# A planner's transfer time, own-result delay and margins renewed, and side work that joins excursions, in a decoder layer

## The chip, the cores and the metric

The kernel runs on one core of a Trainium2 chip. The metric is the device time of one execution in microseconds. Before the change three runs gave 2277.83, 2268.82 and 2278.66 us, with a median of 2277.83 us. One more execution was recorded by the hardware profiler and took 2273.33 us, of which the instructions span 2271.4 us.

## The reference

One decoder layer over 1024 tokens, with 16 learned tokens put in front (1040 columns). All of it is float32.

```python
def swiglu(h, w_gate, w_up, w_down):
    return (jax.nn.silu(h @ w_gate) * (h @ w_up)) @ w_down
...
h = jnp.concatenate([meta, x], axis=1)
n = rms_norm(h, ffn1_norm[l])
h = h + 0.5 * swiglu(n, ffn1_w_gate[l], ffn1_w_up[l], ffn1_w_down[l])
n = rms_norm(h, mix_norm[l])
proj = n @ w_in[l]
...
sb_out = stick_breaking_attention(q, k, v)
rw_out = rwkv7_time_mix(proj[..., 3 * SB_WIDTH:], ...)
h = h + jnp.concatenate([sb_out, rw_out], axis=-1) @ w_out[l]
n = rms_norm(h, ffn2_norm[l])
h = h + 0.5 * swiglu(n, ffn2_w_gate[l], ffn2_w_up[l], ffn2_w_down[l])
return rms_norm(h, final_norm)[:, N_META:]
```

The model width is 1024 and the hidden width of the two feed-forward blocks is 2816. The attention has 8 heads of 64, and so has the recurrence (RWKV-7), which carries a 64 x 64 state per head through all tokens.

## The kernel before

**Tiling.** Activations lie transposed, features on the 128 partitions and tokens along the free axis. The tokens fall into group A (16 learned tokens and the first 512) and group B (the last 512). The long matrix products are the *dense* work: first feed-forward, input projection, output projection, second feed-forward, each for A and then for B. Each float32 product is made of three matmuls in a reduced-precision format (`mm3`, L640): the weight block and the activation are each split into a high and a low part (`whi`, `wlo`; `nh`, `nl`), and high x high, high x low, low x high are summed in PSUM. A weight block comes in by one DMA of 512 KB (`wraw`), ScalarE writes `whi`, and VectorE writes `wlo`. Two such pairs are held at a time, so a new one is split when an old one has been used up. PSUM tiles tell the stage: `pd` is a projection or a down product, `pg` a gate, `pu` (with `nh` and `nl`) an up product, `pwo` the output projection. In the first feed-forward of A and the second of B a part of the products is done in a scheme with fewer multiplications (`quad`), in which the weights also pass through sums on GpSimd.

**Side work.** Beside the dense stream run smaller tasks that also need TensorE: the recurrence and the attention of a group, and the norms. In the recurrence, `lanes` (L1509) inverts small triangular blocks in the steps `pw`, `pp`, `pz`, `pe`. `chain` (L1598) then goes through the token chunks in order; each chunk has a `px<-rsv,x`, a `pu<-us,tt` and a `px<-rsv,bg`, and between two of these ScalarE and VectorE copy a result out of PSUM (into `us`, into `rsv`), without which the next can't start. In the norms, `nps` sums squares and `nyp` spreads the root over the partitions. The attention has `pz`, `pat` and `po`. When TensorE leaves the dense stream for side work, that is called an excursion here.

**What sets the order.** All engines' programs are written out in full when the kernel is built. A planner (`Clock`, L186) keeps a model of the time of each engine and lets tasks go on in the order of the model: the dense task has priority 0, `chain` 9, `lanes` 7, the recurrence's preparation 6 and its end 5, attention 4 to 2, norms 12, weight loads and splits 41 and 40. A task that needs data tells so with `Need` (L141); its `at` (L152) gives the modelled time at which the data are there, plus a margin from `SLACK` (L37) for its priority. `Clock.run` (L400) takes the task that can start first, and at equal times that with the higher priority; the dense task has no margin. Operations of the other engines are held back and committed in the order of the modelled time (`catch_up`, L375; `issue`, L349). So a number of the model changes no instruction, only where each stands in its engine's queue. On the chip each engine works through its queue in that order and waits at an instruction whose data aren't there.

**The output projection of B** needs the recurrence and the attention of B. `plan` (L1225) and `poll` (L2337) put it into the second feed-forward of A, ahead of the first gate that is planned after the data of B are there, or behind that block.

Of the kernel before, what the change touches and what calls it, by code (L numbers as in the profile page):

```python
# [23 lines left out]
NFT = FF // P  # L24
# [9 lines left out]
DB = 2  # L34
WOFF = 1500
NL = 3
SLACK = {9: 0.05, 8: 0.08, 7: 1.5, 6: 0.4, 5: 0.4, 4: 0.4, 3: 0.15, 2: 0.2, 12: 0.1}  # L37
GB = 2
BUFS = [dict(raw=2, qs=4, kh=4, vs=2, sg=8, f=3, at=4, z=2, t=2, o=1),
        dict(raw=1, qs=4, kh=4, vs=2, sg=8, f=2, at=4, z=2, t=2, o=1)]  # L40
WOUT = ((0, 1, 2, 3, 4, 5, 6, 7, 4, 5), (0, 1, 2, 3, 4, 5, 6, 7))
QF = 6
AHEAD = 0.1
BACKLOG = 3.0
PARTS = [(0, 2), (2, 6), (6, 10), (10, 14), (14, 18), (18, 22)]

# [26 lines left out]
class Op:  # L73
# [3 lines left out]
    def at(self):  # L77

        t = self.start
        for d in self.deps:  # L80
            if d.end is None:
                return None
            t = max(t, d.end)
        return t


# [54 lines left out]
class Need:  # L141


    def __init__(self, clk, aps, bank, slack):
        self.clk, self.aps, self.bank, self.slack = clk, [(x.name, Clock.box(x)) for x in aps], bank, slack
        self.both = False

    def __add__(self, t):
        self.slack += t
# [2 lines left out]
    def at(self):  # L152
        t = self.clk.written(self.aps)
        if t is not None and self.bank:
            pool, *ring = self.bank() if callable(self.bank) else self.bank
            f = pool.free(*ring)
            if self.both and f is not None:
                g = pool.free(ring[0], ring[1] - 1)
                f = None if g is None else max(f, g)
            t = None if f is None else max(t, f)  # L160
        return None if t is None else t + self.slack


class Task:
# [21 lines left out]
class Clock:  # L186
# [8 lines left out]
    def __init__(self):  # L195
        self.pe, self.task, self.tasks, self.urg, self.ahead, self.seq = 0.0, None, [], 0, False, 0
        self.clk = dict(v=0.0, a=0.0, g=0.0, s=0.0)
        self.dma = self.port = 0.0
        self.pend = {e: [] for e in self.clk}
        self.wr, self.rd, self.free, self.live, self.held = {}, {}, {}, {}, set()  # L200
        self.mode, self.fast, self.busy = None, True, set()

    @staticmethod
    def box(ap):
# [52 lines left out]
    def cost(self, eng, op, out, ins, k):  # L257

        n = 1
        for d in out.shape[1:]:  # L260
            n *= d
        if eng == "v":
            for x in ins if op == "tensor_reduce" else ():
                n = max(n, x.shape[1] * (x.shape[2] if len(x.shape) > 2 else 1))
            return 0.11 + n * 1e-3 * (2.2 if op == "tensor_tensor_scan" else 8 if op == "reciprocal" else 1.11), 0.17
        if eng == "a":
            far = len(out.shape) > 2 and out.ap[-1][0] * 4 > 64
            return 0.08 + n * 0.84e-3 * (2.2 if far else 1), 0.19
        if eng == "g":
            return ((0.1 + n * 0.85e-3 if op == "memset" else 0.2 + n * 0.9e-3 if op == "affine_select" else 0.22 + n * 1.7e-3), 0.12)  # L270
        if eng == "s":
            big = out if out.space != DRAM or not ins else ins[0]
            m = big.shape[0]
            for d in big.shape[1:]:
                m *= d
            run = min(x.shape[-1] if x.ap[-1][0] == 1 else 1 for x in [out] + ins)
            return 0.3, m * 4 / 2.4e5 * (1 if run >= 128 else 2)
        return self.pe_cost(out, ins, k.get("rhs"), n), 0.23

    def pe_cost(self, out, ins, rhs, n):  # L280
# [20 lines left out]
    def trace(self, eng, op, call, out, ins, k):  # L301
        T = self.task
        o = Op()
        o.eng, o.call, o.task, o.end = eng, call, T, None
        o.cost, o.lat = self.cost(eng, op, out, ins, k)
        lvl = self.LOAD if self.ahead else self.URGENT if self.urg > 0 else self.LAZY if self.urg < 0 else self.PLAIN
        self.seq += 1
        o.port = eng == "g" and op != "memset" or eng == "v" and op.startswith(("tensor_tensor", "scalar_tensor")) and \
            all(x.space != PSUM for x in ins)
        o.prio, o.seq, o.start = (-lvl, -T.prio, self.seq), self.seq, max(self.pe, self.free.get(out.name) or 0.0)  # L310
        deps = {}
        for x in ins:
            b = self.box(x)
            for q, w in self.wr.get(x.name, ()):
                if self.hit(q, b):
                    deps[id(w)] = w
            self.rd.setdefault(x.name, []).append((b, o))
        outs = [out] + [k[n] for n in ("accum_out",) if n in k]
        for x in outs:
            b = self.box(x)  # L320
            if x.space != DRAM:
                for m in (self.wr, self.rd):
                    l = m.get(x.name, ())
                    for q, w in l:
                        if w is not o and self.hit(q, b):
                            deps[id(w)] = w
                    if l:
                        m[x.name] = [(q, w) for q, w in l if w is o or not self.inside(q, b)]
            self.wr.setdefault(x.name, []).append((b, o))
        o.deps = [d for d in deps.values() if eng != "pe" or d.eng != "pe"]  # L330
        o.names = {x.name for x in ins + outs}
        for x in o.names:
            self.live.setdefault(x, []).append(o)
        if eng == "pe":
            for d in o.deps:
                if d.end is None:
                    self.issue(d)
            o.start = max(o.at(), self.pe)
            self.pe = o.start + o.cost
            o.end = self.pe + o.lat  # L340
            o.deps = o.call = None
            T.t = max(T.t, o.end)
            call()
        else:
            self.pend[eng].append(o)
            if not T.free:
                T.ops.append(o)

    def issue(self, o):  # L349
# [7 lines left out]
            self.port = self.clk[o.eng]  # L357
        if o.eng == "s":
            self.dma = max(self.dma, o.start + 0.3) + o.lat
            o.end = max(self.dma, o.start + 0.3 + o.lat) + 1.9  # L360
        else:
            o.end = o.start + o.cost + o.lat
        self.pend[o.eng].remove(o)
# [88 lines left out]
class Ker:  # L452
# [403 lines left out]
    def ffn(self, nm, h, n, chunks, edge, bank, first=None, hook=None, wx=False, poll=None, resid=None, done=None, wy=False, fast=False, once=False):  # L856
# [127 lines left out]
        for part in PARTS:  # L984
            f0, f1 = part
# [48 lines left out]
            if f1 == NFT and hook:  # L1034
                yield from last(part)
            elif not (fast and f1 >= QF):
                for q in range(f1 - f0):
                    yield from downs(part, q)
        for op, x, f in quad_order() if fast else ():
            if op == "d":  # L1040
# [184 lines left out]
    def plan(self):  # L1225

        F = self.flags
# [11 lines left out]
        def ffn(nm, poll=False, wx=False, fast=False, once=False):  # L1239
# [7 lines left out]
            for f0, f1 in PARTS:  # L1247
# [16 lines left out]
                if f1 < NFT:  # L1264
# [1 line left out]
                        F["woutat"] = f1  # L1266
                        yield from wout(True)
                    yield gu("gate", f1)
                yield from [down(f0, f1, q) for q in range(f1 - f0)]
            for op, x, f in quad_order() if fast else ():  # L1270
                if op == "d":
                    yield down(*x, f)
# [785 lines left out]
    def body(self):  # L2058
# [59 lines left out]
        ck, F = self.clock, self.flags  # L2118
# [179 lines left out]
        def director():  # L2298
            yield lambda: F.get("first") and F.get(("xb", 2)) and F.get(("xb", 3)) and F.get(("root", 0, 1)) and F.get("fast1") and psp.quiet()
            psp.release()  # L2300
            for g in range(2):
# [21 lines left out]
                self.ap.release()  # L2323
                self.psa.release()
                F["mix", g] = True
            f2b = f2["p"] = pool("f2b", bufs=1, side="right")
            f2["x"] = self.wx = pool("f2x", bufs=1, side="right")
            ext.extend((pool("psF2", bufs=1, space=PSUM), "e", 6 - DB))
# [144 lines left out]
```

## Time and profile before

| | us |
|---|---|
| three runs | 2277.83, 2268.82, 2278.66 (median 2277.83) |
| profiled execution | 2273.33 |
| its span | 2271.4 |
| DVE (VectorE) busy | 1566.0 (69%) |
| ACT (ScalarE) busy | 1085.4 (48%) |
| POOL (GpSimd) busy | 555.8 (24%) |

In the rows of the profile PE is TensorE, DVE VectorE, ACT ScalarE, POOL GpSimd and SPq the queue that issues DMAs. "L101" is the line of the helper that issues every operation, so instructions are told apart by their tiles, out<-in. PEclk is the share of TensorE's full clock that the chip granted. Matmuls overlap, so what one of them costs is read from start to start, and an idle time of TensorE stands in brackets with what ended it.

### The profile page before, as it was taken

How to read it: one execution, taken by the hardware profiler on the slowest of the kernel's cores; microseconds unless marked ns; L12 is line 12 of the kernel's file. 1: busy time of each engine (PE TensorE's matmuls, PEld its weight loads, DVE VectorE, ACT ScalarE, POOL GpSimd, SP SyncE). 2: the span in 40 equal slices, each digit the busy share in tenths (PEclk: the TensorE clock that was granted, in tenths of full speed). 3: DMA queues.
4: the chain of work that ended last, by engine and by line, in shares of the span. 5: the costliest groups of instructions: out<-in, count | busy, mean ns of one | idle time of the engine just before them, and what ended most of it. 6: DMA issues, size and time to landing. Idle time of an engine off the chain costs nothing.

```text
span 2271.4 us, 41476 instructions
## 1 busy us (share of the span) xinstructions
PE 2239.5 (99%) x16303; PEld 1979.7 (87%) x16303; DVE 1566.0 (69%) x2673; ACT 1085.4 (48%) x2157; POOL 555.8 (24%) x700
## 2 busy tenths in 40 slices
PE   8999999999999999999999999999999999999998
PEld 7999999999878888778788987887877899899998
DVE  6888887475666655676476877547777656688885
ACT  6444444434343534555434554445666335354444
POOL 1322120013133231431012415324443001231110
PEclk9999999999999999999999989999999999999999
DMA  5543332545633233322545524333221433333332
GB/s 166 180 112 103 93 94 78 170 132 145 182 105 106 74 100 98 100 88 67 172 141 175 159 79 128 86 92 116 76 85 52 144 112 126 91 109 109 105 90 78
DMA packets 407384, 256.54 MB, mean 113 GB/s; under 512 B 44941, under 2 KB 392293, under 8 KB 407190
## 3 DMA queue, kind: packets, MB, share of 16 engines
q1 hardware_dynamic: 407190, 253.90, 38.2%
q8 instruction: 128, 2.10, 0.4%
q14 instruction: 66, 0.54, 0.1%
HBM read 219.85 MB, written 33.99 MB: 112 GB/s over the span
## 4 chain that ended last, share of the span: by engine, by line
PE 94%; DVE 2%; ACT 1%; DMA 1%; issue 1%; SPq 0%; POOL 0%; DVEq 0%; ACTq 0%; POOLq 0%
PE pd L101 34%; PE pu L101 22%; PE pg L101 21%; PE pwo L101 4%; PE px L101 3%; PE po L101 2%; PE pz L101 2%; PE pat L101 2%; PE pG L101 1%; DVE wlo L101 1%; PE psw L101 0%; DMA wraw<-in_ffn_w_gate_dram 0%; SPq L101 0%; PE pp L101 0%; ACT whi L101 0%
## 5 line engine op out<-in xcount | busy, mean ns | idle before, releaser
L101 ACT ACTIVATE whi<-wraw 128x1024 fp32r<-128x1024 f32 x314 | 330.6, 1053 | 333.9 <-PE pd L101 208.8
L101 DVE TENSOR_TENSOR wlo<-wraw,whi 128x1024 fp32r<-128x1024 f32 (+1 forms) x312 | 401.0, 1287 | 88.6 <-ACT whi L101 83.8
L101 PE MATMUL pd<-ah,whi 128*128 128x512 f32 (+2 forms) x944 | 325.9, 345 | 2.6 <-DVE h L101 1.2
L101 PE MATMUL pd<-ah,wlo 128*128 128x512 f32 (+2 forms) x944 | 319.3, 338 | 1.2 <-DVE wlo L101 1.2
L101 PE MATMUL pd<-al,whi 128*128 128x512 f32 (+2 forms) x944 | 318.5, 337 | 0.1
L101 PE MATMUL pd<-nh,whi 128*128 128x256 f32 (+7 forms) x648 | 210.6, 325 | 0.3 <-DVE st L101 0.2
L101 PE MATMUL pu<-nh,whi 128*128 128x512 f32 (+3 forms) x576 | 207.0, 359 | 0.0
L101 PE MATMUL pd<-nl,whi 128*128 128x256 f32 (+7 forms) x648 | 204.5, 316 | 0.0
L101 PE MATMUL pd<-nh,wlo 128*128 128x256 f32 (+7 forms) x648 | 204.4, 315 | 0.0
L101 PE MATMUL pg<-nh,whi 128*128 128x512 f32 (+3 forms) x536 | 199.8, 373 | 0.5 <-ACT nh L101 0.5
L101 PEld LDWEIGHTS pd<-ah,whi 128*128 128x128 f32 x944 | 177.6, 188 | 25.5 <-issue 3.1
L101 PE MATMUL pu<-nh,wlo 128*128 128x512 f32 (+3 forms) x576 | 198.6, 345 | 0.6 <-DVE wlo L101 0.6
L101 PE MATMUL pu<-nl,whi 128*128 128x512 f32 (+3 forms) x576 | 198.7, 345 | 0.0
L101 PEld LDWEIGHTS pd<-ah,wlo 128*128 128x128 f32 x944 | 177.6, 188 | 22.5 <-DVE wlo L101 2.1
L101 PEld LDWEIGHTS pd<-al,whi 128*128 128x128 f32 x944 | 177.8, 188 | 17.9 <-DVE al L101 0.7
L101 PE MATMUL pg<-nl,whi 128*128 128x512 f32 (+3 forms) x536 | 190.5, 355 | 0.9 <-DVE nl L101 0.9
L101 PE MATMUL pg<-nh,wlo 128*128 128x512 f32 (+3 forms) x536 | 190.2, 355 | 0.0
L101 POOL TENSOR_TENSOR qs<-wraw 128x512 f32<-128x512 f32 x60 | 101.5, 1697 | 359.3 <-DVE ql L101 142.3
L101 DVE SCALAR_TENSOR_TENSOR h<-pd,h 128x256 f32<-128x256 f32 (+1 forms) x200 | 107.4, 541 | 75.3 <-PE pd L101 73.9
L101 POOL TENSOR_TENSOR al<-sl,ah 128x512 fp32r<-128x512 f32 (+2 forms) x47 | 75.6, 1609 | 323.3 <-ACT ah L101 323.2
L101 PEld LDWEIGHTS pd<-nh,whi 128*128 128x128 f32 (+2 forms) x648 | 120.1, 185 | 13.0 <-issue 3.1
L101 PEld LDWEIGHTS pd<-nh,wlo 128*128 128x128 f32 (+2 forms) x648 | 120.1, 185 | 8.7
(393 smaller groups left out, 5624.6 us busy)
## 6 DMA issues: line engine op xcount, KB each, us to landing
wraw<-in_ffn_w_gate_dram SPq DMA_DIRECT2D x90, 512.0 KB
wraw<-in_ffn_w_up_dram SPq DMA_DIRECT2D x90, 512.0 KB
wraw<-in_ffn_w_down_dram SPq DMA_DIRECT2D x88, 512.0 KB
wraw<-in_w_in_dram SPq DMA_DIRECT2D x54, 512.0 KB
wraw<-in_w_out_dram SPq DMA_DIRECT2D x18, 512.0 KB
s<-rkvd SPq DMA_DIRECT2D x18, 256.0 KB
raw<-qkvd SPq DMA_DIRECT2D x16, 264.0 KB
raw<-qkvd SPq DMA_DIRECT2D x16, 256.0 KB
```

The source lines that it names most:

```text
L101: self._c.trace(self._n, op, lambda: f(*a, **k), out, [x for x in args if isinstance(x, bass.AP)], k)
```

## The change

`SLACK` gets 0.1 us for all priorities from 7 to 2. A new table `JOIN` has a further margin for these priorities (the first set at the start, the second once the attention of group A is over), and it is added only when TensorE's last instruction in the model was not one of a side task. So side work waits longer to begin an excursion, and little to join one. A result that is read on the engine that wrote it counts as there 0.09 us (VectorE) or 0.06 us (ScalarE) sooner. A transfer counts 320 bytes per ns where it was 240, and 1.3 us from its last byte to its reader where it was 1.9. And the output projection of B may also stand between the last down blocks of the second feed-forward of A.

```diff
-SLACK = {9: 0.05, 8: 0.08, 7: 1.5, 6: 0.4, 5: 0.4, 4: 0.4, 3: 0.15, 2: 0.2, 12: 0.1}
+SLACK = {9: 0.05, 8: 0.08, 7: 0.1, 6: 0.1, 5: 0.1, 4: 0.1, 3: 0.1, 2: 0.1, 12: 0.1}
+
+JOIN = ({7: 1.4, 6: 1, 5: 1, 4: 1, 3: 0.5, 2: 1}, {7: 1.4, 6: 0.3, 5: 0.3, 4: 0.3, 3: 0.05, 2: 0.1})
...
+OWN = dict(v=0.09, a=0.06)
...
-            t = max(t, d.end)
+            t = max(t, d.end - OWN.get(self.eng, 0.0) if d.eng == self.eng else d.end)
...
-        self.both = False
+        self.both, self.join = False, clk.joins.get(clk.task.prio, 0.0) if slack and clk.task else 0.0
...
-        return None if t is None else t + self.slack
+        return None if t is None else t + self.slack + (0.0 if self.clk.side else self.join)
...
-            return 0.3, m * 4 / 2.4e5 * (1 if run >= 128 else 2)
+            return 0.3, m * 4 / 3.2e5 * (1 if run >= 128 else 2)
...
+            self.side = T.prio > 0
...
-            o.end = max(self.dma, o.start + 0.3 + o.lat) + 1.9
+            o.end = max(self.dma, o.start + 0.3 + o.lat) + 1.3
...
                 for q in range(f1 - f0):
+                    if poll and q and f1 == NFT:
+                        yield from poll(f1 + q)
                     yield from downs(part, q)
...
-                yield from [down(f0, f1, q) for q in range(f1 - f0)]
+                for q in range(f1 - f0):
+                    if f1 == NFT and q and poll and F.get("f2b") and "woutat" not in F:
+                        F["woutat"] = f1 + q
+                        yield from wout(True)
+                    yield down(f0, f1, q)
...
+                ck.joins = JOIN[1]
```

The set of matmuls is the same before and after (14678 of them); their order isn't. TensorE leaves the dense stream 372 times where it left it 384 times. Three places follow, with the rows of the built programs.

**Place A**, TensorE, where the input projection of group A ends (`pd`) and the first feed-forward of group B begins (`pg`), beside the recurrence's `chain` of group A. Before:

```order
L101 MATMUL pd<-nh_148,whi 128x272
L101 MATMUL pd<-nl_150,whi 128x272
L101 MATMUL pd<-nh_148,wlo 128x272
L101 MATMUL pu<-us,tt 128x64 x2
L101 MATMUL px<-rsv,bg 128x64 x4
L101 MATMUL pg<-nh_147,whi 128x256
L101 MATMUL pg<-nl_149,whi 128x256
```

The same boundary after the change:

```order
L105 MATMUL px<-rsv,bg 128x64 x4
L105 MATMUL pd<-nh_148,whi 128x272
L105 MATMUL pd<-nl_150,whi 128x272
L105 MATMUL pd<-nh_148,wlo 128x272
L105 MATMUL pg<-nh_147,whi 128x256
L105 MATMUL pg<-nl_149,whi 128x256
L105 MATMUL pg<-nh_147,wlo 128x256
```

Before, `px<-rsv,bg` stands right behind the `pu<-us,tt` whose result it needs. Now dense matmuls stand between any two steps of the chain here, and the gate follows the projection at once (nine matmuls of `pg` before the next `px`).

ScalarE at place A, before (`whi<-wraw` is the split of a weight block, `rsv<-pu` the copy for which `px<-rsv,bg` waits):

```order
L101 ACTIVATE us<-px 64x128
L101 ACTIVATE d_7665<-rsv,pc 64x64 x2
L101 ACTIVATE whi<-wraw 128x1024
L101 ACTIVATE rsv<-pu 64x2x64
L101 ACTIVATE whi<-wraw 128x1024
L101 ACTIVATE y<-px 64x2x64 x2
```

ScalarE at place A after the change, one chunk of the chain earlier:

```order
L105 ACTIVATE d_7586<-rsv,pc 64x64 x2
L105 ACTIVATE whi<-wraw 128x1024
L105 ACTIVATE rsv<-pu 64x2x64
L105 ACTIVATE y<-px 64x2x64 x2
L105 ACTIVATE whi<-wraw 128x1024
L105 ACTIVATE d_7664<-rsv,pc 64x64 x2
```

These are the splits of the first gate and the first up block of B. They moved up by one chunk of the chain, and on VectorE the `wlo` of the gate block now stands ahead of the last copy-out of the projection where it stood behind it.

**Place B**, TensorE, where the output projection of group A ends (`pwo`) and the second feed-forward of A begins, beside `lanes` of group B. Before:

```order
L101 MATMUL pp<-lw,tt 32x16 x16
L101 MATMUL pwo<-nh_147,whi 128x256
...
L101 MATMUL nps<-ones,nacc 128x1 x2
L101 MATMUL pz<-t_15294,ab 32x32 x16
L101 MATMUL nps<-ones,nsq 128x1 x2
L101 MATMUL pg<-nh_147,whi 128x256
```

After the change, the first of two such spots:

```order
L105 MATMUL pp<-tt,lw 16x16 x32
L105 MATMUL pp<-lw,tt 32x16 x16
L105 MATMUL pz<-t_15306,ab 32x32 x16
L105 MATMUL pe<-tt,lw 32x32 x16
L105 MATMUL pwo<-nh_147,whi 128x256
```

And the second, about 24 dense matmuls of the gate later:

```order
L105 MATMUL px<-rsv,x_14360 128x64
L105 MATMUL px<-rsv,x_14361 128x64
L105 MATMUL pu<-us,tt 128x64 x2
L105 MATMUL px<-rsv,bg 128x64 x4
L105 MATMUL pu<-nh_147,whi 128x256
```

Before, 24 matmuls of `pwo` stood between `pp` and `pz`, and the norm's `nps` on both sides of `pz`. Now `pp`, `pz` and `pe`, each of which needs the one ahead of it by way of another engine, stand together, and so do three steps of the chain.

**The output projection of B** stands one gate and one up block later than before (ahead of the last gate of the second feed-forward of A, `pg` with f = 21, where it was ahead of f = 20). The new spots between the last down blocks are not used.

More of the change, by code (lines that the diff above doesn't have):

```diff
@@ L200, in __init__ @@
         self.wr, self.rd, self.free, self.live, self.held = {}, {}, {}, {}, set()
-        self.mode, self.fast, self.busy = None, True, set()
+        self.mode, self.fast, self.busy, self.side, self.joins = None, True, set(), False, JOIN[0]
     @staticmethod
```

## The prediction

> **What bounds the kernel now.** I read the engines' busy time first, then the chain that ended last.
>
> ```profile
> PE 2239.5 (99%) x16303; PEld 1979.7 (87%) x16303; DVE 1566.0 (69%) x2673; ACT 1085.4 (48%) x2157; POOL 555.8 (24%) x700
> PE 94%; DVE 2%; ACT 1%; DMA 1%; issue 1%; SPq 0%; POOL 0%; DVEq 0%; ACTq 0%; POOLq 0%
> ```
>
> TensorE is the bound from end to end, and the change neither adds nor removes a matmul. What an order can give or take lies in the 2271.4 - 2239.5 = 31.9 us in which TensorE stands idle, in the cost of changing between dense and side work, and in the clock. So the view of TensorE's waits comes next (line waited for: us in total, times, longest).
>
> ```profile
> PE px L101 <- DVE rsv L101: 3.0, 5, 1.6
> PE nps L101 <- ACT nsq L101: 1.8, 2, 1.2
> PE pgate L101 <- DMA sgl<-lod: 1.1, 1, 1.1
> PE pb L101 <- DVE bg L101: 1.0, 1, 1.0
> PE pp L101 <- issue: 0.9, 2, 0.7
> PE pz L101 <- DVE t L101: 0.8, 1, 0.8
> ```
>
> No wait is large. But the windows view (stretch, its length, busy time of PE, PEld, DVE, ACT, POOL with counts, granted clock, DMA share, GB/s) shows that two of them cost more than they last.
>
> ```profile
> 576.80:580.20 3.40, 3.40 (x27) 3.17 (x26) 1.25 (x6) 1.98 (x7) 0.00 (x0) 1.00 0.57 187
> 580.20:583.60 3.40, 1.76 (x15) 1.66 (x14) 2.01 (x4) 2.66 (x4) 0.00 (x0) 1.00 0.91 296
> 583.60:587.00 3.40, 3.40 (x16) 3.15 (x16) 2.15 (x6) 1.58 (x6) 1.25 (x2) 0.50 1.03 328
> 590.50:593.90 3.40, 3.40 (x18) 3.40 (x17) 2.18 (x5) 0.92 (x3) 0.00 (x0) 0.50 0.16 49
> 593.90:597.30 3.40, 3.40 (x30) 3.27 (x29) 2.36 (x4) 0.42 (x1) 0.30 (x1) 1.00 0.00 0
> 1317.50:1320.90 3.40, 1.67 (x38) 1.23 (x36) 3.30 (x9) 2.69 (x7) 2.00 (x3) 1.00 0.00 0
> 1320.90:1327.70 6.80, 6.19 (x55) 5.90 (x56) 5.42 (x12) 3.12 (x9) 0.00 (x0) 0.50 0.54 152
> 1327.70:1334.50 6.80, 6.80 (x34) 6.80 (x34) 3.77 (x11) 2.57 (x6) 0.00 (x0) 0.50 0.02 4
> ```
>
> Behind each stretch in which TensorE was busy for only half of 3.4 us, its clock was halved: from 583.6 to 593.9 (10.3 us, 5.1 us of work lost) and from 1320.9 to 1334.5 (13.6 us, 6.8 us lost). Those are places A and B. The rest of the span up to 2220 us reads a full clock; the two longest of these stretches:
>
> ```profile
> 60.00:540.00 480.00, 478.75 (x3927) 474.35 (x3927) 354.44 (x616) 218.11 (x415) 90.81 (x116) 1.00 0.41 121
> 600.00:1140.00 540.00, 536.94 (x3552) 434.63 (x3551) 331.15 (x589) 250.61 (x542) 150.63 (x227) 1.00 0.36 103
> ```
>
> So the two places hold about as much as all other waits together.
>
> **The change, part by part.** *Place A.* Timeline rows of TensorE, ScalarE, VectorE and the DMA queue (start, us, engine, what, idle before and what ended it):
>
> ```profile
> 570.37 1.14 SPq L101 DMA_DIRECT2D wraw<-in_ffn_w_gate_dram  x1
> 579.64 0.66 PE L101 MATMUL pu<-us,tt 128*128 128x64 f32 x4
> 580.21 1.06 ACT L101 ACTIVATE whi<-wraw 128x1024 fp32r<-128x1024 f32 x1
> 581.29 0.27 ACT L101 ACTIVATE rsv<-pu 64x128 f32<-64x128 f32 x1
> 581.60 0.28 DVE L101 COPY rsv<-pu 64x128 f32<-64x128 f32 x1 [1.02 <-ACT rsv L101]
> 581.81 1.21 DVE L101 TENSOR_TENSOR wlo<-wraw,whi 128x1024 fp32r<-128x1024 f32 x1
> 581.94 1.10 PE L101 MATMUL px<-rsv,bg 128*128 128x64 f32 x8 [1.64 <-DVE rsv L101]
> 582.85 0.37 PE L101 MATMUL pg<-nh,whi 128*128 128x256 f32 x1
> ```
>
> The gate block was fetched from 570.37 on, but split only at 580.21 to 583.0, behind the last copy-out of the projection, so no dense matmul was there for TensorE. And that split sat on ScalarE just ahead of `rsv<-pu`, for which the chain waited. The new order mends both: the split of the gate stands one chunk earlier, and TensorE has dense matmuls between all steps of the chain. I count the wait of 1.64 us and the lost 5.1 us as gone: **-6.7 us**. What is late next there is the second half of the activations of B, which is loaded while TensorE goes through 48 matmuls and six steps of the chain (some 10 us). The DMA share of 0.91 to 1.03 says that this stretch is full of transfers, so up to 2 us may come back.
>
> *Place B.* Rows of TensorE, VectorE and ScalarE:
>
> ```profile
> 1317.80 0.61 PE L101 MATMUL nps<-ones,nacc 128*128 128x1 f32 x4 [0.17 <-DVE nacc L101]
> 1318.86 0.71 DVE L101 SCALAR_TENSOR_TENSOR t<-pp,half,t 32x128 f32<-32x128 f32 x2
> 1319.25 1.07 PE L101 MATMUL pz<-t,ab 32*32 32x32 f32 x32 [0.84 <-DVE t L101]
> 1321.48 0.78 ACT L101 ACTIVATE lw<-pz 32x256 f32<-32x256 f32 x2
> 1321.51 1.01 PE L101 MATMUL nps<-ones,nsq 128*128 128x1 f32 x4 [1.20 <-ACT nsq L101]
> ```
>
> Before, 0.17 + 0.84 + 1.20 = 2.2 us of waits went ahead of the half clock. In the new order `nps` stands between dense matmuls, so these go. But `pp`, `pz`, `pe` now stand together, and `px`, `pu`, `px` too: `pz` waits for the operation on `t` (0.71 us and its hand-over, an estimate of 0.9), `pe` for the copies of `pz` (0.78, so 1.0), `pu` and `px` for copies of 0.27 and 0.28 in a row (0.6 each). That is 3.1 us, between 0.7 (four times the 0.17 above) and 6.6 (four times the 1.64 of place A): **+0.9 us**. And since the first two waits fall within 3.4 us with only tiny matmuls beside them, I expect the clock to fall here as before: 6.8 us lost before and after, no difference.
>
> [...]
>
> *Excursions.* There are 12 fewer. What one costs beside its own work is read from the first dense matmul behind a `px`:
>
> ```profile
> 576.58 0.37 PE L101 MATMUL pd<-nh,whi 128*128 128x272 f32 x1
> 576.78 0.28 PE L101 MATMUL pd<-nl,whi 128*128 128x272 f32 x1
> 576.90 0.30 PE L101 MATMUL pd<-nh,wlo 128*128 128x272 f32 x1
> ```
>
> It takes 0.20 us to the next start, where 0.12 is usual: 0.08 x 12 = **-1.0 us**, between 0 and -2.
>
> *Smaller margin for joining.* Steps that join have 0.1 us where they had 0.15 to 1.5. At least twelve more join; by the 0.3 us that most lose, TensorE waits 0 to 3.6 us longer. I take **+0.5**, near the low end, since the waits view has few waits of side steps at all.
>
> *The figures for transfers.* Issue of a weight block and its reader:
>
> ```profile
> 1310.92 0.40 SPq L101 DMA_DIRECT2D wraw<-in_ffn_w_gate_dram  x1
> 1314.95 1.06 ACT L101 ACTIVATE whi<-wraw 128x1024 fp32r<-128x1024 f32 x1 [1.63 <-DMA wraw<-in_ffn_w_gate_dram]
> ...
> 1932.27 11.20 PE pd L101 x48
> ```
>
> The third row is from the chain. ScalarE waited for this transfer, so it took 4.0 us. The planner counted 0.3 + 2.2 + 1.9 = 4.4 us for it and now counts 0.3 + 1.6 + 1.3 = 3.2. So it was 0.4 us late and is now 0.8 us early: splits will be written up to 0.8 us too early into ScalarE's queue, and copies of PSUM queue behind them. For dense weights a spare block covers that (24 matmuls of 512 columns, half of the third row, 5.6 us). Without cover are the steps of TensorE that read what a small transfer brought: `pw`, `pp`, `pgate`, two `psw`, five in each of 8 units, 40 in all. Only the waits of `pgate` (1.1) and `pp` (0.9) show now. With 0.6 us less counted, these 40 could give 0 to 24 us; I take **+1.0**, two more such waits of 0.5.
>
> [...]
>
> *The rest.* The wait of `pb` (1.0): the `pG` ahead of it now stand 51 matmuls apart where it was 30, so VectorE has more time; **-0.5**, between -1.0 and 0. The results read on their own engine by 0.09 or 0.06 us sooner only reorder, and are in the rows already. The output projection of B, one gate and one up later, costs nothing: behind it still stand 168 matmuls before the norm of B is needed. The new spots between the last downs aren't used.
>
> **The sum** is -6.7 + 0.9 - 1.0 + 0.5 + 1.0 - 0.5 = **-5.8 us**. Against the profiled execution (2273.33) that gives 2267.5. That execution lies between the fastest (2268.82) and the median of the runs (2277.83); the mean of all four is 2274.7, so I forecast 2274.7 - 5.8 = **2269 us**, 0.4% under the median.
>
> **Rivals.** *Place B doesn't trip the clock.* The waits there are shorter than the 1.64 of place A, and dense matmuls stand closer by. For it: `pgate` waited 1.1 us in one go, and the clock stayed full. Against it: the stretch 1317.5 to 1320.9 tripped with pieces of 0.17 and 0.84 and part of the 1.20. Then another 6.8 us go: 2262. [...]
>
> *Transfers come too late for TensorE (slower).* If the new figures are early by 0.6 us for most small transfers, the steps of `lanes`, `pgate` and `psw` wait. Without my +1.0 the gain is 6.8 us, so from 11 of the 40 waits on it is used up. With 28 of them it is 16.8 - 6.8 = +10 us: 2285. Against it speaks that only three such waits show now, and that steps which begin an excursion have a larger margin.
>
> *Place A trips all the same*, since the second half of the activations arrives late, or a later step does. Then -6.7 falls away: 2276.
>
> *Place B trips twice*, as its two spots are some 15 us apart: 10.3 us more at half clock, 5.1 lost: 2274.
>
> **How the numbers follow.** A run of this kernel differs from no change by what can be told only beyond 0.5%: under 2266.4 or over 2289.2 us. The forecast has 0.45, place B without a trip 0.18, late transfers 0.14, place A all the same 0.13, place B twice 0.10. The four times of before lie within 5 us of their mean; with that scatter a quarter of the forecast's cases are under 2266.4, and four fifths of 2262, a twentieth of the others: 0.11 + 0.14 + 0.01 = 0.26 faster. Slower by over 0.5% are a third of the late transfers, with a little for what I don't see: 0.06. The rest, 0.68, is within 0.5%. From 2257 to 2286 us leaves out some 0.04 of the case at 2262, 0.06 of the one at 2285 and 0.04 of the rest.
>
> **What would show it.** Right: a full clock and no gap at the boundary from `pd` to `pg` near 580 us; `pz` and `pe` near 1315 us each behind an idle time of about 1 us, and a half clock of 10 to 14 us behind them; the wait of `pb` smaller; TensorE's waits in total near 25 us. Wrong: a half clock at a third place, `pg` of B waiting for `nh` or `nl`, or many waits of `pw`, `pp`, `pgate`, `psw` for a DMA.

## The result, and the profile after

The change made the kernel slower. Five executions of the changed kernel have a median of 2292.09 us (2290.91 to 2302.25), five of the kernel before 2274.86 us (2268.82 to 2278.66): a ratio of 1.0089, 95% interval 1.006 to 1.0118. In a later round four more gave 2296.23 us against 2272.65 (1.0105, 1.009 to 1.0119). So the loss is 20 to 24 us, where 6 us of gain were forecast.

The page of the changed kernel, its busy times and the engines' shares of the chain that ended last:

```profile
PE 2250.2 (98%) x16303; PEld 1988.5 (86%) x16303; DVE 1560.0 (68%) x2673; ACT 1085.5 (47%) x2157; POOL 557.6 (24%) x700
PE 83%; DVE 5%; DMA 4%; ACT 3%; issue 2%; SPq 2%; POOL 1%; DVEq 0%; ACTq 0%; POOLq 0%
```

The instructions are as many as before. TensorE's share of the chain went from 94% to 83%, and VectorE, DMA and ScalarE took what it lost. That profile is of the slowest execution (2302.25 us), so I read a second one, of 2294.92 us, taken in run e13. TensorE's waits there between 1215 and 1510 us:

```profile
PE pu L105 <- ACT us L105: 4.0, 4, 1.6
PE pw L105 <- DMA t<-Td: 3.5, 3, 1.2
PE pb L105 <- DVE bg L105: 2.1, 2, 1.9
PE pri L105 <- ACT rw L105: 1.8, 1, 1.8
PE px L105 <- DVE rsv L105: 1.7, 2, 1.2
```

The same part of the kernel before, 1210 to 1495 us:

```profile
PE px L101 <- DVE rsv L101: 1.4, 4, 0.5
PE nps L101 <- ACT nsq L101: 1.2, 1, 1.2
PE pgate L101 <- DMA sgl<-lod: 1.1, 1, 1.1
```

No wait is long; there are more of them, one behind another, and the granted clock was 0.83 from 1330 to 1380 us. The windows view of the second profile at places A and B (the clock stands behind POOL's time):

```profile
540.00:600.00 60.00, 58.10 (x703) 54.35 (x701) 38.41 (x75) 29.44 (x67) 13.44 (x33) 1.00 0.72 211
1330.00:1380.00 50.00, 45.15 (x459) 43.41 (x459) 36.77 (x84) 27.46 (x70) 11.46 (x12) 0.83 0.30 85
```

Place A has a full clock, as forecast. Place B is worse than before. To place the loss I took the start of the dense matmul behind equal amounts of dense work (0.119 us for 256 columns) in this trace and in that of before. Difference after less before, in us, and how much of it is idle time of TensorE and half clock (half its length):

```
dense work      0-360  360-440  440-600(A)  600-1040  1040-1280(B)  1280-1480  1480-end   sum
longer by        +5.9     +3.0        -5.6      +6.5         +14.2       -5.0      +2.7   +21.7
  idle           +2.6     +1.3        +1.6      +2.7          +8.8       -1.2      +1.0   +16.8
  half clock     +5.1        0        -5.1         0          +5.1          0         0    +5.1
```

What is left in a column is side work that stands on the other side of a mark; over the whole it is -0.2. (One excursion at the mark of 1280 moves 1.7 us between its two neighbours; half clock behind the last matmul isn't counted.) So by idle time and half clock alone, place A gained 3.5 us, place B lost 13.9 and the startup 7.7.

### The profile page after: what moved, and what is told of

It is laid out like the page before. It is cut to its first block, busy times and chain, and to the rows that moved or that the text cites. A ratio compares the mean times of both kernels' runs of the same rounds, so it can differ in the third digit from the quotient of the medians.

```text
span 2300.5 us, 41457 instructions
## 1 busy us (share of the span) xinstructions
PE 2250.2 (98%) x16303; PEld 1988.5 (86%) x16303; DVE 1560.0 (68%) x2673; ACT 1085.5 (47%) x2157; POOL 557.6 (24%) x700
## 4 chain that ended last, share of the span: by engine, by line
PE 83%; DVE 5%; DMA 4%; ACT 3%; issue 2%; SPq 2%; POOL 1%; DVEq 0%; ACTq 0%; POOLq 0%
PE pd L105 29%; PE pu L105 20%; PE pg L105 18%; PE pwo L105 3%; PE px L105 3%; PE po L105 2%; PE pz L105 2%; SPq L105 2%; PE pat L105 2%; DVE wlo L105 1%; ACT whi L105 1%; DMA Td<-T 1%; PE pG L105 1%; DMA rkvd<-st 1%; DMA t<-Td 0%
```

## The experiments

Theories: **T**, the early transfer figures cost the time; **M**, the small margins; **O**, own results counted sooner; **S**, the startup; **R**, any new figure draws a new order, and any new order loses. Later came **W** (the place of the output projection of B) and **P** (a few places decide). All runs below compute the whole layer, and mostly only the order differs; in e2, e3, e11 and e12 two weight blocks of the output projection are loaded and split once more (20 transfers of that weight for 18) and TensorE has 8 more small matmuls of the norm (16311 instructions for 16303). In brackets behind a time stand its ratio to the kernel before in the same round and the 95% interval of the ratio.

**Each part alone on the kernel before** (e1 the two transfer figures, e2 `OWN`, e3 `SLACK` and `JOIN`, all without the new spots of the projection).

> The kernel before with only the two figures for transfers renewed; margins, own results and output projection as before. Theory T (the earlier transfer figures cost the time): 10 to 17 us slower than before, with the late startup order of ScalarE that the changed kernel has, and waits of TensorE for DMA or for operands split late. Theory M (smaller margins for joining cost it): within 4 us of before. Theory O (own results counted sooner): within 4 us. Theory R (any new figure re-draws the whole order, and the re-drawn order has waits by chance): anything from -5 to +15 us, and the three parts alone do not add up to +17.

> The kernel before with only the results that an engine reads of its own counted sooner. T: within 4 us of before. M: within 4 us. O: 8 to 17 us slower, with waits of pu, pri, pyT behind ScalarE or VectorE chains. R: anything from -5 to +15 us.

> The kernel before with only the smaller margins and the joining of side steps. M: 8 to 17 us slower, with waits in excursions of several steps (pu behind us, pb behind bg, px behind rsv) and a half clock at place B. T: within 4 us of before. O: within 4 us. R: anything from -5 to +15 us. Its order has 363 excursions where before had 384, so 21 x 0.08 = 1.7 us of changing over is saved in any case.

Measured: e1 2286.8 us (1.005, 1.0035 to 1.0065), e2 2298.15 (1.0108, 1.0091 to 1.0124), e3 2295.89 (1.0097, 1.008 to 1.0114). The three add up to 55 us, the change has 20 to 24. Each of T, M and O expected its own part to be slower, and it was (T in size too, M and O by more than they expected), and was wrong about the other two. But e2 and e3 are poor tests: by the same count as above, 19.6 of the 24.7 us that e2's profile lost and 19.0 of e3's 21.6 lie from 1480 us of dense work on, at the output projection of B (below), where the changed kernel lost 2.7.

**Figures that the change doesn't touch, and the parts turned round.**

```diff
-        return 0.11 + n * 1e-3 * (2.2 if op == "tensor_tensor_scan" else 8 if op == "reciprocal" else 1.11), 0.17
+        return 0.11 + n * 1e-3 * (2.2 if op == "tensor_tensor_scan" else 8 if op == "reciprocal" else 1.11), 0.171
...
-            return 0.3, m * 4 / 2.4e5 * (1 if run >= 128 else 2)
+            return 0.3, m * 4 / 2.41e5 * (1 if run >= 128 else 2)
...
-            o.end = max(self.dma, o.start + 0.3 + o.lat) + 1.9
+            o.end = max(self.dma, o.start + 0.3 + o.lat) + 2.5
...
-SLACK = {9: 0.05, 8: 0.08, 7: 1.5, 6: 0.4, 5: 0.4, 4: 0.4, 3: 0.15, 2: 0.2, 12: 0.1}
+SLACK = {9: 0.06, 8: 0.1, 7: 1.6, 6: 0.5, 5: 0.5, 4: 0.5, 3: 0.2, 2: 0.25, 12: 0.12}
...
-            t = max(t, d.end)
+            t = max(t, d.end + dict(v=0.09, a=0.06).get(self.eng, 0.0) if d.eng == self.eng else d.end)
```

These are e5 (0.18 for 0.171 makes e12), e6, e9, e10 and e11, in this order.

> The kernel before with a figure of the planner that the change does not touch, moved by a thousandth of a microsecond: VectorE's latency 0.171 for 0.17. No theory about the parts of the change says anything of it: T, M and O, within 3 us of before. R (any new figure re-draws the order, and an order that was chosen among many loses by a re-draw): 5 to 23 us slower than before, like the three single parts, with waits in new places. Its order has 385 excursions, one more than before.

> The kernel before with the planner's figure for transfers moved by 0.4% (2.41e5 for 2.4e5), 0.009 us for a weight block; the latency 1.9 stays. T, M and O: within 3 us of before (T by a 130th of the renewal: under 0.1 us). R: 5 to 23 us slower, with waits in new places. 381 excursions.

> The kernel before with the renewal of the transfers turned round: 0.6 us more after each transfer (2.5 for 1.9) where the change takes 0.6 off; the bandwidth stays 2.4e5. In its order 2881 of the 3134 side matmuls stand elsewhere among the dense ones, 9.0 us on average (in the changed kernel 2815 and 4.3 us). Theory T (steps planned too early wait for transfers): no such wait is added, within 4 us of before or up to 5 us faster. Theory R (the order before fits the chip at many places, and any order that is drawn anew loses some of them): 8 to 25 us slower, as the parts of the change, in waits that have nothing to do with transfers.

> The kernel before with all margins of side steps a little larger (0.06, 0.1, 1.6, 0.5, 0.5, 0.5, 0.2, 0.25, 0.12 us for 0.05, 0.08, 1.5, 0.4, 0.4, 0.4, 0.15, 0.2, 0.1): the opposite of the change. 2566 of 3134 side matmuls stand elsewhere, 4.7 us on average. Theory M (smaller margins make side steps wait): less waiting of side steps, within 4 us of before or up to 5 us faster. R: 8 to 25 us slower.

> The kernel before with the results that an engine reads of its own counted 0.09 (VectorE) and 0.06 us (ScalarE) later, the opposite of the change. 2964 of 3134 side matmuls stand elsewhere, 7.2 us on average. Theory O (chains planned too early make TensorE wait): within 4 us of before or up to 5 us faster. R: 8 to 25 us slower.

> The kernel before with VectorE's latency in the planner 0.18 for 0.17 us, a figure that the change leaves alone and by 6% only. 2449 of 3134 side matmuls stand elsewhere, 4.8 us on average, where the two neutral edits tried so far moved 12 and 78 and were no test of a new draw. T, M, O: within 4 us of before. R: 8 to 25 us slower.

Measured: e5 2273.2 us (1.0004, 0.9991 to 1.0017) and e6 2272.49 (0.9988, 0.9979 to 0.9998), whose edits moved 12 and 78 side matmuls and so were no test of R; e9 2281.08 (1.0043, 1.0029 to 1.0057), e10 2278.18 (1.0027, 1.0017 to 1.0036), e11 2304.21 (1.014, 1.012 to 1.016), e12 2290.48 (1.0083, 1.0062 to 1.0104). Turned round, every part of the change is slower as well (e10 by less than R's range), and so is a figure that has nothing to do with it. So the direction of the figures doesn't decide, T, M and O fall as the cause of the whole, and R stood so far. Here too the output projection of B is in the sum: from 1480 us on e11 lost 19.7 of its 32.8 us and e12 19.2, while the rest of e12 was 5 us shorter than before.

**The changed kernel with one part undone.** e4 keeps the old transfer figures while the planner's TensorE time is under 30 us:

```diff
-m * 4 / 3.2e5 *
+m * 4 / (2.4e5 if self.pe < 30.0 else 3.2e5) *
-o.lat) + 1.3
+o.lat) + (1.9 if self.pe < 30.0 else 1.3)
```

e7 has `OWN = dict()`; e8 has the old `SLACK` and an empty `JOIN`.

> The changed kernel, but the old figures for transfers hold while the planner's time on TensorE is under 30 us, which brings back the startup order of ScalarE and VectorE from before. Theory S (the startup holds a part of the loss): the wait of pxn falls from 4.7 to under 2 us and its difference to before at the first dense matmuls goes, 3 to 8 us faster than the changed kernel; the rest of the loss stays (9 to 14 us slower than before). If the startup is not a part of it: within 2 us of the changed kernel, 15 to 19 us slower than before. R: the rest of the order is re-drawn in places too, so up to 5 us either way beside that.

> The changed kernel without the earlier own results. O (they cost 23 us as in the run of that part alone): 15 to 23 us faster than the changed kernel. R: the parts do not add up, anything from -10 to +10 us of the changed kernel, so 7 to 27 us slower than before.

> The changed kernel with the old margins and without joining. M (smaller margins cost 20.8 us as in the run of that part alone): 14 to 21 us faster than the changed kernel, and the waits in excursions of several steps gone. R: anything from -10 to +10 us of the changed kernel, so 7 to 27 us slower than before.

Measured: e4 2291.48 us (1.0072, 1.0057 to 1.0088), e7 2286.5 (1.0057, 1.0042 to 1.0072), e8 2288.98 (1.0067, 1.0052 to 1.0082). By the ratios, e4, e7 and e8 are 4, 7 and 5 us faster than the changed kernel in its first runs (1.0089), and 7, 11 and 9 us in those of e13 (1.0105). (The intervals of all three overlap that of the first runs and lie under that of e13's.) No part holds the whole. Of the 15 to 23 us that O and the 14 to 21 us that M expected, neither came.

**The startup.** e13 is the changed kernel again; e14 is e1 with the edit of e4.

> The changed kernel unaltered, for a second profile, since its first profile is of its slowest execution (2302.25, median 2292.09). If the waits of its order are its own: the same waits of pu behind us (6.0 us), pxn behind xn (5.6), pri, pw, pb near 1300 us again, and only the clock or a few transfers differ, 2291 to 2293 median. If the first profile was a bad execution: the waits near place B or in the startup are smaller by some 10 us in total.

> The kernel before with the new transfer figures, the old ones kept while the planner's TensorE time is under 30 us. Against the run with the transfer figures alone (2286.8) only the order of the startup differs. Theory S (the startup is most of what the transfer figures cost): 6 to 8 us faster, 2279 to 2281. If the startup costs nothing, as the run of the changed kernel with the old startup said (0.6 us): 2286 to 2288.

Measured: e13 as above, with nearly the same waits as the first profile, but 2296.23 us where 2291 to 2293 were expected. e14 2277.2 us (1.0022, 1.0012 to 1.0031), 9.6 us under e1 (by the ratios 6.4) and a little under the range expected. Only 48 side matmuls of the startup differ, so S holds: over half of what the transfer figures cost is the startup. The timeline there, VectorE and GpSimd of the changed kernel (e13), of the kernel before, and of e14:

```profile
11.53 5.56 DVE L105 TENSOR_SCALAR xn<-xn,bst 128x1024 f32<-128x1024 f32 x2
11.44 2.35 POOL L105 TENSOR_TENSOR wlo<-wraw,whi 128x1024 fp32r<-128x1024 f32 x1 [9.91 <-ACT whi L105]
13.73 2.81 POOL L105 TENSOR_TENSOR wlo<-wraw,whi 128x1024 fp32r<-128x1024 f32 x1
```

```profile
10.55 1.41 DVE L101 TENSOR_SCALAR xn<-xn,bst 128x1024 f32<-128x1024 f32 x2
11.42 5.10 POOL L101 TENSOR_TENSOR wlo<-wraw,whi 128x1024 fp32r<-128x1024 f32 x2 [9.90 <-ACT whi L101]
```

```profile
11.30 1.42 DVE L105 TENSOR_SCALAR xn<-xn,bst 128x1024 f32<-128x1024 f32 x2
12.18 5.12 POOL L105 TENSOR_TENSOR wlo<-wraw,whi 128x1024 fp32r<-128x1024 f32 x2 [10.65 <-ACT whi L105]
```

The early transfer figures put `h<-px` ahead of the squares `xq<-xt` on ScalarE; the norm's root is 1 us later; and then VectorE begins its two operations on `xn` 0.09 us behind GpSimd's split where it began 0.87 us ahead. Then they take 5.56 us, for 1.41. TensorE waits 4.8 us for `xn`, and its clock falls for 10.2 us (e13, and the kernel before, where it doesn't):

```profile
12.80:23.00 10.20, 7.65 (x32) 6.75 (x33) 8.84 (x13) 7.07 (x12) 3.74 (x2) 0.50 0.36 105
```

```profile
12.80:23.00 10.20, 8.53 (x72) 7.92 (x71) 7.79 (x17) 6.25 (x10) 3.73 (x2) 1.00 0.48 141
```

GpSimd's two operations ended at 13.79 and 16.54 us, and VectorE's (2.80 and 2.84 us) at 14.33 and 17.09: each 0.55 us behind one of GpSimd's. So the rows show VectorE slow beside a GpSimd operation that had begun before its own; by what means isn't shown.

**The output projection of B.** In e2, e3, e11 and e12 it stands behind the last downs of the second feed-forward of A; before and in the changed kernel it stands among its gates and ups. e15 is e12 with the change's new spots.

> The kernel before with VectorE's latency 0.18 (2290.5 in its run), and with the change's new spots for the output projection of B between the last downs. Its order differs from that run only there: the projection stands behind the first of the last downs, with 72 matmuls of downs after it, where it had none. Theory W (a projection behind the last downs makes TensorE wait for the norm and the weight splits, 18 to 19 us with the half clock): 16 to 20 us faster than that run, 2270 to 2275, level with the kernel before or up to 4 us faster. If the projection's place costs nothing, as the prediction had it: 2288 to 2293.

Measured: 2282.56 us (1.0037, 1.0024 to 1.005), 7.9 us under e12 (by the ratios 10.5); expected were 16 to 20. TensorE's waits from 1880 to 1940 us in e12, then in e15, and the clock in each:

```profile
PE pwo L101 <- DVE wlo L101: 6.1, 2, 5.3
PE pu L101 <- DVE wlo L101: 4.4, 1, 4.4
```

```profile
PE pd L101 <- DVE wlo L101: 1.9, 1, 1.9
PE pu L101 <- DVE wlo L101: 1.3, 2, 0.7
```

```profile
1890.00:1935.00 45.00, 35.21 (x266) 34.80 (x265) 28.67 (x61) 19.20 (x37) 9.11 (x11) 0.85 0.32 98
```

```profile
1890.00:1935.00 45.00, 41.81 (x293) 38.39 (x292) 32.29 (x77) 27.09 (x60) 12.12 (x14) 1.00 0.39 117
```

VectorE in e12, ahead of the first of these waits:

```profile
1895.39 1.27 DVE L101 SCALAR_TENSOR_TENSOR nf<-h2B,vec,ny 128x256 f32<-128x256 f32 x3
...
1898.99 2.35 DVE L101 TENSOR_TENSOR wlo<-wraw,whi 128x1024 fp32r<-128x1024 f32 x2
```

With nothing dense left of A, the norm of B (`nf`, `nacc`, `n2Bl`) fills VectorE, `wlo` is split behind it, and TensorE waits long twice. Two of the ten blocks of the projection that e12 splits here are loaded a second time; the kernel before splits eight. From 1480 us of dense work on, e12 lost 19.0 us to the kernel before and e15 6.1: the move, with the two blocks less that come with it, is worth 13 us there. The rest of what was expected isn't the place: in the part before it, where both have the same order, e15's profile lost 8.5 us more to the half clock.

**The places against the draw.** Three edits of the kernel before, e16, e17 and e18:

```diff
-            return 0.08 + n * 0.84e-3 * (2.2 if far else 1), 0.19
+            return 0.08 + n * 0.84e-3 * (2.2 if far else 1), 0.195
...
-            o.end = max(self.dma, o.start + 0.3 + o.lat) + 1.9
+            o.end = max(self.dma, o.start + 0.3 + o.lat) + 2.0
...
-SLACK = {9: 0.05, 8: 0.08, 7: 1.5, 6: 0.4, 5: 0.4, 4: 0.4, 3: 0.15, 2: 0.2, 12: 0.1}
+SLACK = {9: 0.05, 8: 0.08, 7: 1.5, 6: 0.5, 5: 0.5, 4: 0.5, 3: 0.2, 2: 0.3, 12: 0.1}
```

> The kernel before with ScalarE's latency in the planner 0.195 for 0.19 us. Its order differs little (988 side matmuls, 0.6 us on average), but at place A the last steps px, pu and px stand apart, with dense matmuls between. The prediction's term for place A (the wait of 1.64 us and the half clock of 5.1 us go): 5 to 7 us faster than before, 2266 to 2268 where before has 2273, and no half clock near 584 us. If the clock falls there all the same: within 2 us of before. Theory R taken literally (any new draw loses): 5 us slower or more.

> The kernel before with 2.0 for 1.9 us after each transfer in the planner. 1955 of 3134 side matmuls stand elsewhere, 2.7 us on average; startup and output projection of B stand as before; pu and px, which stood together at place A, stand 0.8 us of dense matmuls or more apart, and no other two steps of one chain stand together. Theory P (the loss of an order is at its places: steps of a chain together, startup, projection behind the last downs): as fast as the run with place A mended, 3 to 7 us faster than before, 2265 to 2270 where before has 2272.5. Theory R (any new draw loses): 5 to 20 us slower.

> The kernel before with margins of 0.5 for 0.4 us (three kinds of steps), 0.2 for 0.15 and 0.3 for 0.2. 2183 of 3134 side matmuls stand elsewhere, 3.2 us on average; startup and output projection of B as before; at place A px, px, pu, px, px stand in a row without a dense matmul (before: two steps), and at place B pp and pz. Theory P: four waits of 1.0 to 1.6 us where before had one of 1.6, and about 10 us of half clock as before: 3 to 6 us slower than before at place A, up to 2 at place B, 2275 to 2281. Theory M (larger margins make less waiting): 2 to 5 us faster. R: 5 to 20 us slower.

Measured: e16 **2266.51 us** (0.9975, 0.9966 to 0.9984), 6.1 us faster than before; e17 2268.29 (0.9983, 0.9971 to 0.9996), 4.5 faster; e18 2280.68 (1.0031, 1.0021 to 1.0042), 7.9 slower. R in its strong form falls: e17 draws two thirds of the side work anew and gains. Clock at place A: before, e16, e17, e18.

```profile
540.00:600.00 60.00, 58.24 (x685) 55.84 (x684) 38.95 (x82) 26.87 (x64) 5.91 (x5) 0.91 0.59 174
```

```profile
540.00:600.00 60.00, 57.35 (x697) 54.47 (x696) 38.56 (x82) 27.12 (x66) 5.50 (x5) 0.97 0.63 183
```

```profile
540.00:600.00 60.00, 58.42 (x725) 55.19 (x723) 42.81 (x82) 28.12 (x66) 6.53 (x9) 1.00 0.62 184
```

```profile
540.00:600.00 60.00, 57.96 (x676) 55.36 (x676) 37.75 (x79) 26.90 (x66) 5.87 (x7) 0.91 0.61 179
```

P got the totals right, but partly by luck. By stretch, e16's profile gained 1.7 us at place A and 3.6 at place B, e17's 3.3 and 2.9. In e18 the five steps in a row at place A lost nothing (-0.6 us from 440 to 600 of dense work). Its loss is at place B, 11.8 us from 1040 to 1280: 6.0 more idle time and 6.8 more half clock, in four stretches. The longest single wait is where `pp` and `pz` stand together:

```profile
1317.55 0.33 DVE L101 SCALAR_TENSOR_TENSOR t<-pp,half,t 32x128 f32<-32x128 f32 x1
1317.93 0.31 PE L101 MATMUL pz<-t,ab 32*32 32x32 f32 x2 [3.47 <-DVE t L101]
1318.22 0.35 DVE L101 SCALAR_TENSOR_TENSOR t<-pp,half,t 32x128 f32<-32x128 f32 x1 [0.34 <-ACT tt L101]
```

`t` takes 0.33 us, but VectorE was full of the norm of A (`nf`, `nl`, `nacc`) until 1317.5, so `pz` waited 3.5 us. So in e18 steps that join cost little at place A, and 3.5 us at once where the helping engine had other work.

## Why the prediction was wrong

**The step that failed is "the rest".** It took the places whose rows I had compared and let all others stand as before. But 2815 of the 3134 side matmuls stood elsewhere among the dense ones, 4.3 us on average, and new waits appeared at places that have no term in the sum: 7.7 us of idle time and half clock in the startup, 1.3 from 360 to 440, 2.7 from 600 to 1040, and some 6.7 of idle time around place B at steps that I hadn't compared. The old order had few such waits, and nothing in the new figures keeps what it had. Beside that, the terms of the two places were mis-sized. Point by point, from the second profile:

- *Place A, -6.7*: right in its mechanism, too large by about 3. The half clock and the old wait are gone, but the idle time there rose by 1.6 in all (a wait of 1.9 of a down product, `pd<-ah`, among the new ones), so 3.5 us came of it where 6.7, less up to 2, were counted on. The price of a half clock is a part of that: e17 as a whole has 6.8 us less of half clock (half its length) and 0.2 less idle time, and is 4.3 shorter; e18 has 6.8 more and 4.7 more idle time, and is 8.4 longer. So there half the length overstates it.
- *Place B, +0.9 and no difference in the clock*: mis-sized. It lost 13.9 us, 8.8 idle and 5.1 half clock. At the two spots whose rows I had compared the four waits came to 4.3 us (0.9 at `pz`, 0.6 at `pe`, 1.6 at `pu`, 1.2 at `px`) where 3.1 were forecast; the rest of the idle time is `pw`, `pb`, `pri` and others nearby. The rival that it trips twice was the true one in price (10.2 and 6.8 us of half clock, from 1333.7 and 1354.2 on, and two of 3.4 ahead of them: 5.1 us lost more than before), though two executions of nearly one order can differ by as much (last section).
- *Excursions, -1.0*: nothing of this size can be told apart; what is neither idle nor clock sums to -0.2.
- *Smaller margin, +0.5*: too small in company. Undone in the changed kernel (e8), the margins are worth 0.0022 to 0.0038 by the ratios, 5 to 9 us; added to the transfer figures alone (e1 to e7) under 2, which is within the intervals.
- *Transfers, +1.0*: the mechanism was there, and mis-sized: seven waits of TensorE for a transfer, 5.4 us, of `pw`, `psw` and `pp` in e13 (the break-even of 11 waits wasn't reached, its 6.8 us nearly). Splits queued too early on ScalarE, which I had named and left at nothing, cost too; one of them is shown below. What they cost in all isn't shown: ScalarE's waits for weight blocks at `whi` went from 13.4 us to 17.8. e14 puts the figures without the startup at 4.6 us, and the startup, at which I had not looked, at 6 to 10 more.
- *The wait of `pb`, -0.5*: the wrong sign, 1.0 became 2.1.
- *Own results, 0*: wrong. Undone (e7) they are worth 7 to 11 us by the ratios.
- *Output projection, 0*: right for this order, where the new spots aren't used; but in e12 a spot of this kind is worth 8 to 13 us.

Of the signs that I had named, the full clock at place A came; a half clock at a third place came too (the startup), and so did a longer wait of `pb` and waits of `pw` for a DMA. Two slips in the working change nothing: the fastest of the four times lies 5.9 us under their mean, not within 5, and a twentieth of the other cases is 0.02, not 0.01.

The same count for the parts, idle time and half clock together, in us more than before:

```
dense work            0-360  360-440  440-600(A)  600-1040  1040-1280(B)  1280-1480  1480-end
e1, transfers          +4.7     +1.7        -7.8      +5.3          +5.3       -1.2       0.0
e14, without startup   +1.0     +2.5        -7.9      +5.7          +4.2       -1.2       0.0
e2, own results        -0.1      0.0        -0.8      +1.2          +7.7       -1.2     +17.8
e3, margins            -0.9     -0.1        -2.7      +2.8          +6.4       -1.0     +17.9
e13, the change        +7.7     +1.3        -3.5      +2.7         +13.9       -1.2      +1.0
e8, no margins         +7.6     +2.7        -5.1      +3.3          +4.3       -1.2      +0.9
e7, no own results    +12.0     +1.6        -5.1      +2.8          -0.3       -0.7      +2.9
```

The loss from 360 to 440 and the gain at place A come with the transfer figures alone, and most of the loss from 600 to 1040 does. At place B each part alone loses 4 to 8 us and the change 14; without own results (e7) it has 4.8 us more idle time there than before, where the change has 8.8, and 5.1 less half clock, which by itself varies that much; its startup is 4 us worse. (In e1 the clock is on record only from 25.9 us on, so its startup may hold half clock that isn't counted here.)

How a split queued too early becomes a wait of TensorE, in e13 (DMA queue, ScalarE, TensorE):

```profile
1305.32 0.39 SPq L105 DMA_DIRECT2D wraw<-in_w_out_dram  x1
1310.67 1.06 ACT L105 ACTIVATE whi<-wraw 128x1024 fp32r<-128x1024 f32 x1 [4.22 <-DMA wraw<-in_w_out_dram]
1311.63 0.40 ACT L105 ACTIVATE nsq<-h 128x256 f32<-128x256 f32 x1
1311.94 0.61 ACT L105 ACTIVATE rw<-rt 128x512 f32<-128x512 f32 x1
1312.60 0.66 PE L105 MATMUL pri<-ident,rw 128*128 128x128 f32 x4 [1.81 <-ACT rw L105]
```

The block took 5.35 us from issue to split where the planner now counts 3.2. ScalarE stood for 4.2 us at the split, `rw` behind it, and TensorE waited 1.8 us for `rw`. The wait of `pb` has another cause, like that in the startup: its `bg` stood behind a `wlo` that took 2.94 us beside a GpSimd operation begun 0.05 us earlier.

```profile
1265.85 1.92 POOL L105 TENSOR_TENSOR bk<-bk,pe 128x1024 f32<-128x1024 f32 x1 [27.11 <-PE pG L105]
1265.90 2.94 DVE L105 TENSOR_TENSOR wlo<-wraw,whi 128x1024 fp32r<-128x1024 f32 x1
1269.76 0.42 DVE L105 TENSOR_TENSOR bg<-pG,maskG 128x256 f32<-128x256 f32 x1
1270.33 1.02 PE L105 MATMUL pb<-blk,prod 128*128 128x2 f32 x8 [1.93 <-DVE bg L105]
```

The `wlo` of the kernel before at 581.81 us, beside which GpSimd stood idle, took 1.21 us.

The figure for own results is no error in itself, by this pair. Two dependent operations of VectorE in e13:

```profile
10.36 0.16 DVE L105 SCALAR_TENSOR_TENSOR bst<-bst 128x2 f32<-128x2 f32 x1
10.55 0.16 DVE L105 TENSOR_TENSOR bst<-bst 128x2 f32<-128x2 f32 x1
```

They start 0.19 us apart. By the code the planner counted 0.11 + 0.002 + 0.17 = 0.28 us, and with 0.09 off it counts 0.19. My reading, which is only argued, is that the old 0.09 us were a margin in each link of a chain, for stalls that the planner doesn't know (a GpSimd operation alongside, a late block). The change took it away together with the margins of `SLACK`. No run tests this reading; the figure turned the other way (e11) was slower as well.

What stays open: how the three parts together make 14 us at place B, since no run mends that place alone; and whether e16 and e17 gain at place B by their order. Their half clock there is 6.8 us shorter than before, but e5, whose order there is practically that of before and whose time is the same, has 10.2 us less of it too.

## What to carry to other kernels

A change of a planner's figure isn't the sum of the places where one sees it: ask first how much of the order it draws anew, and then look at every place where a chain of small steps meets a busy helper engine (startup, boundaries between stages, a block with nothing dense left behind it). A truer figure can make the kernel slower, as that for own results did here (by my reading, which no run tests, because the old error was a margin); so renew a figure by small steps, each with a timed run: the orders drawn here ranged from 6 us faster to 33 slower. And one profile isn't enough to price a half clock: practically the same order showed 3.4 and 13.7 us of it in the same place.

## What the runs showed of the hardware

The half clock varies between executions of one order. At place B, where TensorE's order is the same in both, the kernel before had it for 13.7 us and e5 for 3.4 (in the first of its two rows):

```profile
1320.00:1335.00 15.00, 13.80 (x110) 13.40 (x104) 10.15 (x24) 6.02 (x16) 0.67 (x2) 0.54 0.25 71
```

```profile
1303.00:1320.00 17.00, 15.29 (x258) 14.73 (x258) 14.38 (x31) 8.25 (x19) 3.78 (x5) 0.90 0.44 113
1320.00:1335.00 15.00, 13.84 (x167) 13.13 (x166) 14.11 (x37) 10.81 (x30) 2.45 (x4) 1.00 0.27 77
```

From 1320 us on TensorE has the same busy time in both, with 110 and 167 matmuls. The changed kernel itself had 34.1 us of half clock in e13 up to the last matmul and 44.4 in its first profile. In the profile of the kernel before all changes of the clock lie on one grid of 3.413 us (from 583.63 us on, at 3, 216, 220 and 493 steps: 593.87, 1320.91, 1334.56 and 2266.40), and so do the 15 changes in the first profile of the changed kernel, from 13.59 us on. In the two profiles of the changed kernel the grid lies 0.83 us apart against the start of the program. So where a step of the grid cuts a cluster of waits differs; that this is what decides is argued, not shown.

Half a step of work isn't what decides either, as I had read it from the two places before (1.76 and 1.67 of 3.40 us). The clock halved behind a step with 2.44 of 3.40 us of work (e13, the first two rows), and stayed full behind one with 1.81 of 3.41 (the first profile of the changed kernel, the last two):

```profile
1330.30:1333.70 3.40, 2.44 (x132) 1.98 (x130) 2.06 (x6) 2.34 (x6) 3.26 (x5) 1.00 0.03 5
1333.70:1337.10 3.40, 2.77 (x39) 2.57 (x40) 3.40 (x3) 2.80 (x10) 1.95 (x1) 0.50 0.32 91
1317.47:1320.88 3.41, 1.81 (x16) 1.81 (x17) 2.66 (x6) 3.26 (x7) 0.00 (x0) 1.00 0.08 23
1320.88:1324.29 3.41, 3.23 (x30) 3.15 (x28) 2.53 (x5) 1.09 (x3) 0.00 (x0) 1.00 0.59 177
```

In the startup, VectorE's operation on `xn` took 0.7 us where it began ahead of GpSimd's split (before) and 2.8 where it began behind it (e13). Its start had moved by 0.96 us against that of the split, and TensorE's wait for it went from 1.7 us to 4.8.
